# A hybrid decoder layer on one core: odd heads' probability scales and all ALiBi biases moved to the scalar engine

## The chip, the cores and the metric

The kernel runs on one core of a Trainium2 chip. The metric is the device time of one execution in microseconds (us), as the median of several runs. Engines are named as in the profile: PE is TensorE (matmuls; its weight loads are listed as PEld), DVE is VectorE, ACT is ScalarE, POOL is GpSimd, SP is SyncE, which issues the DMAs.

## What is computed

One decoder layer on x of 512 tokens by 1024 features, in float32. Cut to its steps:

```
h = rmsnorm(x, attn_norm)
mq, mk, mv, rq, rk, rv, rg = split(h @ w_in)             # 7 parts of 512 columns
moba = block-sparse causal attention(mq, mk, mv)         # 8 heads of 64, blocks of 256 keys
       softmax(q k^T / 8 - slope_h * distance) @ v       # slope_h = 2^-(h+1), h = 0..7
ret  = chunkwise retention(rq, rk, rv)                   # 4 heads of 128, decay per head
ret  = head_groupnorm(ret) * silu(rg)
x = x + concat(moba, ret) @ w_out
h = rmsnorm(x);  u = causal conv of width 3 (h @ w_up)   # 2816 wide
x = x + (gelu(u) * (h @ w_gate)) @ w_down
x = x + (p @ w_ple) * sigmoid(rmsnorm(x) @ w_ple_gate)
out = rmsnorm(x, final_norm)
```

With 512 tokens there are two blocks of 256 keys, so that every query sees all keys up to its own.

## The kernel before

Activations are kept transposed, features on partitions and the 512 tokens along the free axis. Every float32 product is made of three float32r matmuls: each operand is split into a rounded part `hi` and the remainder `lo`, and `mm3` issues hi·hi (L93), hi·lo of the moving side (L94) and lo·hi (L95). Operand names ending in `h` and `l` are the two parts.

A weight comes by DMA as a raw tile `wr`, ACT rounds it into `wh` (L152), and the remainder `wl = wr - wh` is made on POOL for the keys mv, rq, rk, rg, mq, mk and out, on DVE for the others (L153, L154). The `wh` and `wl` buffers are four each, so a `wh` waits until PE is through with the weight that had its buffer.

`project` (L359) makes one 128-feature tile of a projection: 24 matmuls into a PSUM tile `pj`, a scaling copy `pt` on DVE (L366), then a split, `hi` on ACT (L75) and `lo` on DVE (L82).

Retention goes head by head. `ret_scores` (L408) makes four score tiles; each is multiplied by its decay on DVE (`rt`, L420), rounded on ACT (L422) and the remainder made on DVE (L423). The last tile of a head goes into two fixed tiles called `corner`, the others into `rh` and `rl`. `ret_values` (L426) multiplies them with the values into `ro`.

MoBA goes through g = 0 to 3, two heads each (e = 0 and 1, so that head h is 2g + e), with two blocks b of queries each and two steps in each block: sixteen steps, in which the score rows of both heads have 128, 256, 384 or 512 keys. `softmax` adds the bias and takes the minimum of the negated row in one DVE instruction (`ml`, L458, listed as CUSTOM_DVE_ANT_0), Exp and the row sum on ACT (L461; `me` are the probabilities, `mt` the sum), the reciprocal on DVE (`mi`, L463), and scales the probabilities by it on DVE, in place (L464). `moba_turn` then transposes the probabilities on PE into a PSUM tile `mp` and splits it, `hi` on ACT (L512), `lo` on DVE (L513); the tiles on the diagonal go into other fixed `corner` tiles, the rest into `mph` and `mpl`. `moba_values` multiplies them with the values into `mo`, and adds the two halves through a copy `mr` on ACT (L530) and a sum `mt` on DVE (L531).

The bias of a head is `base`, a tile of distances, times 2^-(h+1): one instruction of 128x512 on POOL (L453). The biases of heads 0 and 1 are issued in the second round of the retention loop, after its three projections (L629 to L631), and those of heads 2g + 2 and 2g + 3 at the end of `moba_scores` for block 0 of g.

Between the steps the schedule puts other work of PE as a fill: projections, and products of the output projection `ou` (L610 to L668). The order of PE's instructions is fixed as written, by a dependency of each on the one before (L843 to L850). The orders on DVE, ACT and POOL are made by the scheduler of the tile framework, which estimates durations and moves an instruction ahead of another that is expected to be ready later. Each engine then works through its list in that order. Eight PSUM tiles and 76 tiles of 128x512 in the on-chip memory are handed out in turn, so an instruction may also wait until a tile's last reader is through.

Of the kernel before, what the change touches and what calls it, by code (L numbers as in the profile page):

```python
# [13 lines left out]
AF = mybir.ActivationFunctionType  # L14
ALU = mybir.AluOpType
# [26 lines left out]
def hybrid_layer_kernel(ctx, tc, x, p, attn_norm, w_in, ret_norm, w_out, ffn_norm, w_up, w_gate,  # L42
                        conv_w, conv_b, w_down, ple_norm, w_ple, w_ple_gate, final_norm, decay, out):
    nc = tc.nc
# [15 lines left out]
    def h2k(s, dt=F32):  # L60

        return heap.tile([P, T], dt, tag="b2k", name=nm(s))
# [4 lines left out]
    def sm(s, n=4, dt=F32):  # L67
        return small.tile([P, n], dt, tag=f"sm{n}", name=nm(s), bufs=12)
# [255 lines left out]
    base = h2k("base")  # L324
# [7 lines left out]
    for kk in range(4):  # L332
# [13 lines left out]
        for h in range(HR):  # L346
            nc.vector.tensor_scalar(c[:, h * DR:(h + 1) * DR], a[:, h * DR:(h + 1) * DR], mean[:, h:h + 1], None,
                                    op0=ALU.subtract)
# [100 lines left out]
    biases, probs, probsT, pair = {}, {}, {}, {}  # L449

    def moba_bias(h):
        biases[h] = h2k("bias")
        nc.gpsimd.tensor_scalar(biases[h], base, 2.0 ** -(h + 1), None, op0=ALU.mult)  # L453

    def softmax(s, h, qt, e):
        keys = P * (qt + 1)
        least = sm("ml", 1)
        nc.vector.tensor_tensor_reduce(e, s[:, :keys], biases[h][:, T - keys:], scale=-1.0,  # L458
                                       scalar=3.4e38, op0=ALU.add, op1=ALU.min, accum_out=least)
        total = sm("mt", 1)  # L460
        nc.scalar.activation(e, e, AF.Exp, bias=least, scale=-1.0, accum_out=total)  # L461
        inv = sm("mi", 1)
        nc.vector.reciprocal(inv, total)  # L463
        nc.vector.tensor_scalar(e, e, inv, None, op0=ALU.mult)  # L464

    def moba_scores(g, b, step):
        q, (kh, kl) = qs["mq", g], qs["mk", g]
        if step == 0:
            probs[g, b] = {}
            if b == 0:  # L470
                pair[g] = [h2k("me") for _ in range(2)]
        pr, both = probs[g, b], pair[g]
        for qt in (2 * b + step,):
            keys = P * (qt + 1)
            wide = max(keys, 256)
            ss = [ps("ms") for _ in range(2)]
            own = slice(qt * P, (qt + 1) * P)
            for e in range(2):
                nc.tensor.matmul(ss[e][:, :wide], q[e][:, own], kh[e][:, :wide], start=True, stop=False)
                nc.tensor.matmul(ss[e][:, :wide], q[e][:, own], kl[e][:, :wide], start=False, stop=True)  # L480
            for e in range(2):
                if b == 0:
                    pr[e, qt] = both[e][:, qt * P:qt * P + keys]
                else:
                    pr[e, qt] = h2k("me")[:, :keys]
                softmax(ss[e], 2 * g + e, qt, pr[e, qt])
        if step == 0:
            return
        if b == 1:
            del qs["mq", g], qs["mk", g], pair[g]  # L490
            for e in range(2):
                del biases[2 * g + e]
        elif g + 1 < HM // 2:
            for e in range(2):
                moba_bias(2 * g + 2 + e)
# [122 lines left out]
    for h in range(HR):  # L618
        ret_scores(h)
        project(*tiles[3 * h])  # L620
        ret_values(h)
        if h == 0:
            moba_v(3)
        if h:
            ret_gate(h - 1)
        project(*tiles[3 * h + 1])
        ret_sums(h)
        project(*tiles[3 * h + 2])
        if h == 1:  # L629
            for e in range(2):  # L630
                moba_bias(e)  # L631
# [172 lines left out]
    for c in range(2):  # L804
        for t in range(NT):
# [24 lines left out]
            else:  # L830
                nc.scalar.activation(o[0], x3[t, 0], AF.Copy, scale=r4)
                for q in range(2):
                    v = slice(q * 256, (q + 1) * 256)
                    nc.vector.scalar_tensor_tensor(o[1][:, v], x3[t, 1][:, v], r4, fn[1][:, v],
                                                   op0=ALU.mult, op1=ALU.mult)
# [49 lines left out]
```

## Time and profile before

| | us |
|---|---|
| median of three runs | 703.02 |
| lowest and highest run | 702.95, 703.88 |
| the profiled execution | 702.89 |
| its span in the trace | 700.9 |
| mean granted PE clock | 0.994 |
| PE busy | 682.1 |
| DVE busy | 435.1 |
| ACT busy | 284.5 |
| POOL busy | 125.0 |

The span goes from the first to the last instruction of the trace; 2.0 us of the execution's time lie around it. A busy time is the sum of an engine's instructions. PE's clock is given as a share of its full speed: 1.00 is the upper of its two levels, 0.50 the lower. Durations of single instructions overlap a little, since the next one starts before the last result of the one before is written.

### The profile page before, as it was taken

The page shows a single profiled execution, that of the slowest core. Times are in us where ns is not written, and L with a number is a line of the kernel's source. Part 1 is how long each engine was busy: PE and PEld are TensorE (multiplying, and loading weights), DVE is VectorE, ACT ScalarE, POOL GpSimd, SP SyncE. Part 2 cuts the span into 40 slices and gives each one's busy share as a digit, 9 for nine tenths or more (in the row PEclk, how much of TensorE's full clock was granted, in tenths as well). Part 3 has the DMA queues.
Part 4 walks back from the last instruction along what each step waited for, and adds up shares of the span by engine and source line. Part 5 has one row for each costly group of instructions (what it writes and reads, how often), then busy time and mean ns, then how long its engine had stood idle before and what let it go on. Part 6 is the DMA issues. An engine that isn't in the chain of part 4 may idle for free.

```text
span 700.9 us, 8468 instructions
## 1 busy us (share of the span) xinstructions
PE 682.1 (97%) x3200; PEld 568.5 (81%) x3200; DVE 435.1 (62%) x785; ACT 284.5 (41%) x460; POOL 125.0 (18%) x99
## 2 busy tenths in 40 slices
PE   8999999999998999999999999999999999999995
PEld 6888888888776888888888888888888888888884
DVE  5776687766768766775656653234565565466496
ACT  5534633335455764453433431222343343344311
POOL 5236244425425210000000000000000000000145
PEclk9999999999999999999999999999999999999998
DMA  8334422245953012232331222233323212344003
GB/s 269 126 93 133 131 80 75 61 124 147 277 142 92 1 62 59 64 118 75 105 121 60 91 90 91 91 120 121 99 82 121 74 62 75 113 146 163 1 1 120
DMA packets 73390, 71.38 MB, mean 102 GB/s; under 512 B 2450, under 2 KB 62726, under 8 KB 73350
## 3 DMA queue, kind: packets, MB, share of 16 engines
q1 hardware_dynamic: 73190, 70.58, 33.3%
q8 instruction: 25, 0.41, 0.3%
q10 hardware_dynamic: 160, 0.27, 0.1%
q14 instruction: 15, 0.12, 0.1%
HBM read 62.97 MB, written 2.10 MB: 93 GB/s over the span
## 4 chain that ended last, share of the span: by engine, by line
PE 87%; DVE 5%; DMA 2%; ACT 2%; issue 2%; POOL 1%; SPq 0%; DVEq 0%; ACTq 0%; POOLq 0%
PE gate L93 6%; PE gate L95 6%; PE up L95 6%; PE dn L94 6%; PE dn L95 6%; PE gate L94 6%; PE up L93 6%; PE up L94 6%; PE dn L93 6%; PE pj L93 4%; PE pj L94 4%; PE pj L95 4%; PE ou L93 2%; PE ou L95 2%; PE ou L94 2%
## 5 line engine op out<-in xcount | busy, mean ns | idle before, releaser
L152 ACT ACTIVATE wh<-wr 128x1024 fp32r<-128x1024 f32 (+2 forms) x108 | 105.3, 979 | 206.6 <-PE dn L94 57.3
L154 DVE TENSOR_TENSOR wl<-wr,wh 128x1024 fp32r<-128x1024 f32 (+2 forms) x78 | 84.6, 1086 | 45.6 <-ACT wh L152 45.5
L154 POOL TENSOR_TENSOR wl<-wr,wh 128x1024 fp32r<-128x1024 f32 x30 | 73.4, 2447 | 130.0 <-ACT wh L152 130.0
L93 PE MATMUL gate<-h2h,wh 128*128 128x512 f32 x176 | 68.7, 390 | 0.0
L95 PE MATMUL gate<-h2h,wl 128*128 128x512 f32 x176 | 68.5, 389 | 0.0
L94 PE MATMUL gate<-h2l,wh 128*128 128x512 f32 x176 | 68.5, 389 | 0.0
L93 PE MATMUL up<-h2h,wh 128*128 128x512 f32 x176 | 68.5, 389 | 0.0
L94 PE MATMUL up<-h2l,wh 128*128 128x512 f32 x176 | 68.5, 389 | 0.0
L95 PE MATMUL up<-h2h,wl 128*128 128x512 f32 x176 | 68.5, 389 | 0.0
L93 PE MATMUL dn<-ach,wh 128*128 128x512 f32 x176 | 68.5, 389 | 0.0
L94 PE MATMUL dn<-acl,wh 128*128 128x512 f32 x176 | 68.5, 389 | 0.0
L95 PE MATMUL dn<-ach,wl 128*128 128x512 f32 x176 | 68.5, 389 | 0.0
L93 PE MATMUL pj<-h1h,wh 128*128 128x512 f32 x160 | 63.3, 395 | 0.3 <-DVE corner L513 0.3
L94 PE MATMUL pj<-h1l,wh 128*128 128x512 f32 x160 | 62.4, 390 | 0.0
L95 PE MATMUL pj<-h1h,wl 128*128 128x512 f32 x160 | 62.4, 390 | 0.0
L711 POOL MEMSET u<- 128x2 f32 x22 | 2.1, 100 | 316.4 <-DVE c L718 316.4
L722 DVE TENSOR_TENSOR ga<-gate,r2b 128x512 f32<-128x512 f32 x22 | 15.2, 691 | 41.3 <-PE gate L95 41.3
L712 DVE TENSOR_TENSOR u<-up,r2b 128x512 f32<-128x512 f32 x22 | 15.1, 692 | 40.1 <-PE up L95 40.1
L94 PEld LDWEIGHTS up<-h2l,wh 128*128 128x128 f32 x176 | 33.0, 188 | 6.9
L93 PEld LDWEIGHTS dn<-ach,wh 128*128 128x128 f32 x176 | 33.0, 188 | 6.9
L94 PEld LDWEIGHTS dn<-acl,wh 128*128 128x128 f32 x176 | 33.0, 188 | 6.9
L95 PEld LDWEIGHTS gate<-h2h,wl 128*128 128x128 f32 x176 | 33.0, 188 | 6.9
(234 smaller groups left out, 1416.0 us busy)
## 6 DMA issues: line engine op xcount, KB each, us to landing
wr<-in_w_up_dram SPq DMA_DIRECT2D x11, 1024.0 KB, 5.4
wr<-in_w_gate_dram SPq DMA_DIRECT2D x11, 1024.0 KB, 5.4
wr<-in_w_in_dram SPq DMA_DIRECT2D x20, 512.0 KB, 4.0
wr<-in_w_down_dram SPq DMA_DIRECT2D x8, 768.0 KB, 4.3
wr<-in_w_down_dram SPq DMA_DIRECT2D x8, 640.0 KB, 4.1
wr<-in_w_ple_gate_dram SPq DMA_DIRECT2D x4, 1024.0 KB, 4.9
wr<-in_w_out_dram SPq DMA_DIRECT2D x3, 1024.0 KB, 6.2
xn<-in_x_dram SPq DMA_DIRECT2D x8, 256.0 KB, 5.8
```

Of the source, the lines that this page charges most:

```text
L93: nc.tensor.matmul(acc, a[0], b[0], start=first, stop=False)
L94: nc.tensor.matmul(acc, a[0], b[1], start=False, stop=False)
L95: nc.tensor.matmul(acc, a[1], b[0], start=False, stop=last)
L152: nc.scalar.activation(hi, part, AF.Copy)
L154: (nc.gpsimd if aside else nc.vector).tensor_tensor(lo, part, f(hi), op=ALU.subtract)
L711: nc.gpsimd.memset(u[:, 0:2], 0.0)
L712: nc.vector.tensor_tensor(u[:, 2:], up, r2b, op=ALU.mult)
L722: nc.vector.tensor_tensor(ga, gate, r2b, op=ALU.mult)
```

## The change

`moba_bias` makes the bias by an ACT copy with a scale in place of a POOL multiplication, for all eight heads. In `softmax` the heads with odd h (e = 1) scale their probabilities by an ACT copy, with the reciprocals as the scale of each row; the even heads keep the DVE multiplication. So one scale of each of the sixteen steps moves from DVE to ACT, four each of 128, 256, 384 and 512 columns. No data, tile or DMA is added. Lines behind L464 stand three lines further down in the changed kernel (the L512 of before is L515).

```diff
     def moba_bias(h):
         biases[h] = h2k("bias")
-        nc.gpsimd.tensor_scalar(biases[h], base, 2.0 ** -(h + 1), None, op0=ALU.mult)
+        nc.scalar.activation(biases[h], base, AF.Copy, scale=2.0 ** -(h + 1))
...
         inv = sm("mi", 1)
         nc.vector.reciprocal(inv, total)
-        nc.vector.tensor_scalar(e, e, inv, None, op0=ALU.mult)
+        if h % 2:
+            nc.scalar.activation(e, e, AF.Copy, scale=inv)
+        else:
+            nc.vector.tensor_scalar(e, e, inv, None, op0=ALU.mult)
```

PE's and SP's lists are the same before and after. ACT's and DVE's lists change in order too. Three places follow, all on ACT; a row with + is of the changed kernel alone, one with - of the kernel before, the others of both.

First, ACT in the third head of the retention (`rh`, and `corner_610` for its last score tile); `wh_1408` is a weight of a later projection:

```order
 L369 ACTIVATE sil_1159<-pt_1157 128x512
+L453 ACTIVATE bias_1161<-base_419 128x512
+L453 ACTIVATE bias_1163<-base_419 128x512
 L422 ACTIVATE rh_1173<-rt_1171 128x512
 L422 ACTIVATE rh_1183<-rt_1181 128x384
 L422 ACTIVATE rh_1193<-rt_1191 128x256
+L152 ACTIVATE wh_1408<-wr_1268 128x1024
 L422 ACTIVATE corner_610<-rt_1201 128x128
-L152 ACTIVATE wh_1408<-wr_1268 128x1024
 L75 ACTIVATE rqh_1236<-pt_1234 128x512
```

The two biases are new ahead of `rh_1173`, and `wh_1408` has moved ahead of `corner_610`. On DVE, at the same place, the copy `pt_1234` of a projection has moved ahead of `corner_611`, the remainder that belongs to `corner_610`.

Second, ACT at the change from g = 0 to g = 1 of MoBA: `me_1781` are probabilities of head 1, `me_1839` and `me_1840` those of heads 2 and 3, `corner_602` a turned tile, `wh_2116` a weight of the output projection:

```order
 L152 ACTIVATE wh_2112<-wr_2008 128x1024
 L461 ACTIVATE me_1781,mt_1784<-me_1781,ml_1782 128x512
-L512 ACTIVATE corner_602<-mp_1941 128x384
+L465 ACTIVATE me_1781<-me_1781,mi_1786 128x512
+L515 ACTIVATE corner_602<-mp_1941 128x384
 L461 ACTIVATE me_1839,mt_1849<-me_1839,ml_1847 128x128
 L461 ACTIVATE me_1840,mt_1856<-me_1840,ml_1854 128x128
 L75 ACTIVATE mqh_1890<-pt_1886 128x512
+L465 ACTIVATE me_1840<-me_1840,mi_1858 128x128
+L152 ACTIVATE wh_2116<-wr_2110 128x1024
 L461 ACTIVATE me_1839,mt_1906<-me_1839,ml_1904 128x256
-L152 ACTIVATE wh_2116<-wr_2110 128x1024
```

Two scales are new, ahead of `corner_602` and behind `mqh_1890`, and `wh_2116` has moved ahead of an Exp of 256 columns. DVE's list has at this place, before and after, the reciprocal that needs this Exp ahead of the minimum of `me_1840`.

Third, ACT in the first two steps of g = 2: `me_2154` and `me_2155` are probabilities of heads 4 and 5, `corner_606` a turned tile, `mr_2248` a copy in `moba_values`:

```order
+L465 ACTIVATE me_2155<-me_2155,mi_2173 128x128
 L461 ACTIVATE me_2154,mt_2221<-me_2154,ml_2219 128x256
-L530 ACTIVATE mr_2248<-mo_2237 64x256
+L453 ACTIVATE bias_2233<-base_419 128x512
+L453 ACTIVATE bias_2235<-base_419 128x512
+L533 ACTIVATE mr_2248<-mo_2237 64x256
 L152 ACTIVATE wh_2768<-wr_2336 128x1024
 L461 ACTIVATE me_2155,mt_2228<-me_2155,ml_2226 128x256
-L512 ACTIVATE corner_606<-mp_2286 128x384
```

The next row of ACT after these is `corner_606` in the changed kernel as well (L515). A scale and two biases are new ahead of it, the biases ahead of `wh_2768` too.

## Rows read from the trace of the kernel before

**Rows 1.** The page, part 1: each engine's busy us, share of the span, instructions

```profile
PE 682.1 (97%) x3200; PEld 568.5 (81%) x3200; DVE 435.1 (62%) x785; ACT 284.5 (41%) x460; POOL 125.0 (18%) x99
```

**Rows 2.** PE's waits: line waited for, us in total, times, longest

```profile
PE ou L93 <- DVE corner L513: 3.1, 1, 3.1
PE ou L93 <- DVE ml L458: 1.7, 1, 1.7
...
PE mo L522 <- DVE mpl L513: 1.2, 1, 1.2
```

**Rows 3.** Groups by line and shape: busy us, mean ns, idle before and its releasers

```profile
L464 DVE TENSOR_SCALAR me<-me,mi 128x384 f32<-128x384 f32 x8 | 3.4, 424 | 0.0
...
L461 ACT ACTIVATE me<-me,ml 128x512 f32<-128x512 f32 x8 | 5.8, 719 | 4.4 <-DVE ml L458 3.5 <-DVE me L464 0.9
L461 ACT ACTIVATE me<-me,ml 128x384 f32<-128x384 f32 x8 | 4.9, 616 | 4.1 <-DVE ml L458 3.8 <-DMA mq<-mqh 0.3
...
L461 ACT ACTIVATE me<-me,ml 128x128 f32<-128x128 f32 x8 | 3.2, 401 | 4.1 <-DVE ml L458 4.1
```

**Rows 4.** Timeline of 115 to 124 us (retention): start, us, instruction, idle before

```profile
115.11 2.40 POOL L154 TENSOR_TENSOR wl<-wr,wh 128x1024 fp32r<-128x1024 f32 x1 [1.06 <-ACT wh L152]
...
116.26 1.80 DVE L423 TENSOR_TENSOR rl<-rt,rh 128x512 fp32r<-128x512 f32 x1 [0.70 <-ACT rh L422]
...
120.89 0.39 PE L94 MATMUL pj<-h1l,wh 128*128 128x512 f32 x1
...
121.28 0.31 ACT L422 ACTIVATE corner<-rt 128x128 fp32r<-128x128 f32 x1 [0.75 <-DVE rt L420]
...
121.49 1.04 ACT L152 ACTIVATE wh<-wr 128x1024 fp32r<-128x1024 f32 x1
...
121.62 0.29 DVE L423 TENSOR_TENSOR corner<-rt,corner 128x128 fp32r<-128x128 f32 x1 [0.44 <-ACT corner L422]
...
122.61 2.40 POOL L154 TENSOR_TENSOR wl<-wr,wh 128x1024 fp32r<-128x1024 f32 x1 [5.11 <-ACT wh L152]
...
123.03 0.28 PE L94 MATMUL ro<-corner,rvh 128*128 128x256 f32 x1
```

**Rows 5.** Timeline of 181 to 192 us (first MoBA steps)

```profile
182.58 2.36 POOL L154 TENSOR_TENSOR wl<-wr,wh 128x1024 fp32r<-128x1024 f32 x1 [7.86 <-ACT wh L152]
...
183.44 1.78 DVE L464 TENSOR_SCALAR me<-me,mi 128x512 f32<-128x512 f32 x1
...
187.83 0.51 ACT L461 ACTIVATE me<-me,ml 128x256 f32<-128x256 f32 x1 [0.22 <-DVE ml L458]
...
188.55 0.40 DVE L458 CUSTOM_DVE_ANT_0 me<-ms,bias 128x256 f32<-128x256 f32 x1
...
189.53 2.41 POOL L154 TENSOR_TENSOR wl<-wr,wh 128x1024 fp32r<-128x1024 f32 x1 [1.40 <-ACT wh L152]
...
189.85 0.40 PE L93 MATMUL pj<-h1h,wh 128*128 128x512 f32 x1
...
190.41 0.56 DVE L513 TENSOR_TENSOR corner<-mp,corner 128x384 fp32r<-128x384 f32 x1
```

**Rows 6.** Timeline of 212 to 222 us (MoBA, g = 2)

```profile
213.51 2.95 POOL L453 TENSOR_SCALAR bias<-base 128x512 f32<-128x512 f32 x2
...
215.58 0.68 DVE L82 TENSOR_TENSOR mql<-pt,mqh 128x512 fp32r<-128x512 f32 x1
...
216.92 2.50 DVE L464 TENSOR_SCALAR me<-me,mi 128x256 f32<-128x256 f32 x1
216.93 2.35 POOL L154 TENSOR_TENSOR wl<-wr,wh 128x1024 fp32r<-128x1024 f32 x1 [0.47 <-ACT wh L152]
...
217.38 0.49 ACT L512 ACTIVATE corner<-mp 128x384 fp32r<-128x384 f32 x1
...
219.80 0.55 DVE L513 TENSOR_TENSOR corner<-mp,corner 128x384 fp32r<-128x384 f32 x1
```

**Rows 7.** A stretch behind the longest wait: us, PE, PEld, DVE, ACT, POOL, clock, DMA, GB/s

```profile
220.80:224.20 3.40, 3.40 (x10) 2.62 (x9) 2.86 (x7) 2.40 (x5) 1.28 (x1) 0.50 0.89 294
```

## The prediction

> **What bounds the kernel now.** I read the page first: PE is busy 682.1 us, 97% of the span, 3200 matmuls [rows 1]. So PE paces, and an edit on ACT, DVE or POOL counts only where PE comes to wait, or stops waiting. The waits of PE, read next, are few, and the largest three lie in MoBA: 3.1 us for a `corner` lo part, 1.7 us for a softmax minimum, 1.2 us for a turned lo part [rows 2]. The change can take away at most these 6.0 us. What they pull after them is read from the table by stretches: behind the 3.1 us wait PE's granted clock stands at half speed for 3.4 us [rows 7]. Behind the 1.7 and 1.2 us waits I found no such stretch. A stretch of 3.4 us at half speed does 1.7 us of work, so the large wait costs 3.1 + 1.7 = 4.8 us. Last come the timelines around each wait and around the places where the order of instructions changes: the reader is to see there which engine releases PE, and what that engine did just before.
>
> The rows show a second thing: while POOL works on a weight's lo part, some DVE instructions stand still. The retention's `rl` (512 columns, both inputs in SBUF) was listed at 116.26 beside POOL's `wl` of 115.11 to 117.51 and took 1.80 us [rows 4]; a DVE subtraction of the same size with both inputs in SBUF took 0.68 [rows 6]. A probability scale of 256 columns took 2.50 us beside a `wl` [rows 6], one of 512 took 1.78 [rows 5]. Each ended within some 0.6 us of POOL's end. A `corner` lo part that subtracts from PSUM was not held: it took 0.56 at 190.41, inside POOL's `wl` of 189.53 to 191.94 [rows 5].
>
> **The change part by part.** A new price first: an ACT scale by a per-row factor. The nearest rows are ACT's own Exp of the same sizes: 0.40 us for 128 columns, 0.62 for 384, 0.72 for 512 [rows 3]; I take these. On DVE 384 columns took 0.42 [rows 3]. A bias of 512 columns on ACT is priced by plain copies: 0.31 us for 128 columns [rows 4], 0.49 for 384 [rows 6], so about 0.58 for 512; I take 1.1 for a pair. In all 16 scales leave DVE, one in each step, four of each size, and 8 biases leave POOL.
>
> That each scale is dearer on ACT costs 0.62 − 0.42 = 0.19 us at 384 columns, 16 × 0.19 = 3.0 us if every one lay on PE's path. ACT was busy 41% of the span [rows 1], so I cost the scales at nothing except at the places below; if that cover were gone, 3.0 us is the price. The Trainium skill, page "ScalarE: Activation LUTs", section "Rules for kernel authors", speaks against the change: a multiplication belongs on VectorE, up to about three times faster per element in bf16. The trace has 1.45 times (0.62 against 0.42, in float32); at three times the estimate for the 16 would be 6.6 us instead of 3.0.
>
> *Retention, 121 to 125 us: +2.1.* The first two biases now stand on ACT ahead of `rh_1173` (first piece of the order, above). They cost nothing: `rl`, which needs `rh`, could start at 116.26 but stood held by POOL until 117.51 [rows 4], which covers 1.25 us, and the pair is 1.1. If that `wl` were not there, the pair would reach DVE in full, 1.1 us. The dear part is the exchange of `wh_1408` and `corner_610`. Before, `corner` hi ran at 121.28, `wh` behind it at 121.49, POOL's `wl` at 122.61, and the lo part at 121.62 on DVE was through before POOL began [rows 4]. Now `wh` comes first. It needs its buffer, free when PE's product of 120.89 ends (121.28), so it runs 121.3 to 122.3; POOL's `wl` starts 0.1 behind it, about 122.4, as 122.61 stands to 121.49 + 1.04 [rows 4]. `corner` hi then runs 0.31 and ends near 122.6, and DVE's lo part, two SBUF inputs, comes about 0.2 us behind POOL's start: held until 122.4 + 2.4 = 124.8, done at about 125.1. PE's product with it was due at 123.03 [rows 4]: 2.1 us late. Ends: 0 (it slips in ahead of POOL) and 2.3 (`wh` starts 0.2 later, at 121.49 as before). I take 2.1, since POOL is ahead by most of the estimates. A wait of 2.1 lies nearer 1.7 (clock kept) than 3.1 (clock lost), so I add nothing for the clock; the other end is +1.7.
>
> *First MoBA steps, 181 to 192: −0.5.* The DVE scale at 183.44, held 1.78, is an odd head's and goes; with it goes the 1.7 us wait [rows 2, 5]. But ACT now holds that scale (0.7) ahead of `corner` hi, another of 128 columns (0.4), and `wh_2116` (1.04) ahead of the Exp of 256 columns (second piece). That Exp ran at 187.83; DVE's next reciprocal waits for it, and behind that on DVE stands the other head's minimum of 188.55, which gives PE a PSUM bank for the projection started at 189.85 [rows 5]. The delays sum to 0.7 + 0.4 + 1.0 = 2.1; the slack is 189.85 − 188.95 = 0.9. So a new wait of 1.2 takes the place of 1.7. Ends: −1.7 (no new wait) and +0.4 (no slack). I take −0.5.
>
> *The turned lo part near 197: +0.2.* Its 1.2 us wait [rows 2] is for a split that ends behind DMAs out of `mq`, and two biases (1.1) now stand on ACT just ahead of that. Ends 0 and +1.1; I take 0.2, nearer nothing, because a DMA ends that wait and not ACT.
>
> *217 to 220: −0.5.* DVE's even-head scale of 216.92 was held by the `wl` of 216.93, and `corner` lo stood behind it until 219.80, though its hi part had begun at 217.38 [rows 6]. Now two biases and a scale stand on ACT ahead of `wh` (third piece), so `wl` starts some 1.1 later and that DVE scale runs before it, unheld. `corner` hi however comes behind the biases, the `wh` and an Exp: 217.38 + 1.1 plus 0.3 to 0.6 for the scale and for gaps begins near 218.9; its lo part, which reads PSUM and so is not held, follows near 219.35 in place of 219.80 [rows 6], some 0.5 earlier. Ends: −3.1 (ACT hides all) and +0.6 (a whole scale more). With the wait still at 2.6, nearer 3.1 than 1.7, I leave the clock's 1.7 us in on both sides.
>
> *The rest: +0.2.* The other twelve or so scales and the other biases meet PE without waits in the rows; one `corner` late in MoBA comes behind an ACT scale. Ends 0 and 1.0.
>
> The sum: +2.1 − 0.5 + 0.2 − 0.5 + 0.2 = +1.5. The profiled execution took 702.89, so 704.4; the median of the runs stands 0.13 above it, so **704.5**. Some 0.2% of the time, 1.4 us, is what a measurement can tell from no change.
>
> **The rivals.**
>
> *A, DVE gets in first at 122.6.* Then POOL is the one that waits, the 2.1 us are gone: 704.5 − 2.1 = 702.4. For it: the margin is 0.2 us. Against it: at 216.92 DVE was listed 0.01 ahead of POOL and was held all the same [rows 6].
>
> *B, the clock stays up at 217* because the idle stretch shrinks from 3.1 to 2.6: 704.5 − 1.7 = 702.8. The rows have a fall behind 3.1 and none behind 1.7; 2.6 lies between.
>
> *C, the clock falls at 123 as well*, behind 2.1 us of idle PE: 704.5 + 1.7 = 706.2. The same rows leave it open.
>
> *D, ACT paces MoBA.* If half of the 16 scales lie on PE's path, 1.5 us more: 706.0. For it: in each step ACT must now do Exp, Exp and scale before the turn. Against it: ACT is busy 41% [rows 1].
>
> *E, faster: the emptied queues clear 217.* If `corner` hi gets ahead of the biases there, it starts at about 217.4, PE waits some 1.5 instead of 3.1 and the clock stays up: −1.6 − 1.7. If the first steps also keep slack, −1.7 in place of −0.5. With the +2.1 of retention and 0.4 of small terms, 703.0 − 1.6 − 1.7 − 1.7 + 2.1 + 0.4 = 700.5. It decides where `corner` hi begins: before 217.6 or not. The order now puts it behind the biases, which speaks against. That freeing POOL of biases frees DVE as well would speak for it, but a subtraction with two SBUF inputs ran in 0.68 at 215.58, inside POOL's biases of 213.51 to 216.46 [rows 6]. The Trainium skill, page "SBUF — State Buffer", section "SBUF: two separate sides", has DVE and GpSimd exclude each other for a whole instruction, for any GpSimd operation that reads SBUF. By it that subtraction would have been held; the trace disagrees for the biases and agrees for `wl`. If it held for the biases too, E would deserve more.
>
> That the change does not do what it says is excluded: the order shows the instructions on ACT, none on the old engines.
>
> **How the numbers follow.** Chances: the forecast 0.40, A 0.15, B 0.13, C 0.12, D 0.10, E 0.10. The forecast's own range is 703.8 to 705.2, so its lower half, 0.18, falls within 1.4 us of the time before, its upper half, 0.22, beyond. Same: 0.18 + A + B = 0.46. Slower: 0.22 + C + D = 0.44. Faster: E, 0.10. The range goes from A to C, 702.4 to 706.3; it leaves out E and the tails of A and D.
>
> **What would show it.** Right: a new wait of about 2 us of PE for the DVE `corner` of the retention near 123, with POOL's `wl` beside that instruction; the 1.7 us wait gone and one of about 1.2 for a minimum in its place near 188; the 3.1 us wait at 2.4 to 2.8, half speed behind it; ACT busy some 14 us more, POOL 12.1 less; ACT scales near 0.4 to 0.7 us. Wrong: no wait at 123; a wait at 217 below 2 us; the clock at half speed elsewhere; or waits of PE for ACT in most steps.

## The result, and the profile after

The change makes the kernel slower: 707.88 us median of six runs (706.15 to 710.79) against 702.99 for the kernel before, a ratio of 1.0070 with a 95% interval of 1.0047 to 1.0093. Measured once more later (e4 below) it took 706.09 us, a ratio of 1.0050 (1.0027 to 1.0074). The forecast was 704.5, with a range up to 706.3: the sign of its sum is right, its size, +1.5, is too small against the +4.9 measured here and the +3.8 of e4. One of the eight runs of e9 (below) took 2385.30 us at a mean granted clock of 0.28 and is left out of e9's median.

The page of the changed kernel, part 1, against [rows 1]: PE has 2.7 us more of busy time, with the same matmuls; DVE and POOL lost 9.5 and 12.3 us, ACT gained 10.6.

```profile
PE 684.8 (97%) x3200; PEld 571.4 (81%) x3200; DVE 425.6 (60%) x769; ACT 295.1 (42%) x484; POOL 112.7 (16%) x91
```

The new instructions' groups, by line and shape. The prices taken from the Exp rows were right: 0.39, 0.61 and 0.72 us for 128, 384 and 512 columns [rows 3].

```profile
L453 ACT ACTIVATE bias<-base 128x512 f32<-128x512 f32 x8 | 4.6, 617 | 0.0
L465 ACT ACTIVATE me<-me,mi 128x512 f32<-128x512 f32 x4 | 2.9, 722 | 0.3 <-DVE mi L463 0.2
L465 ACT ACTIVATE me<-me,mi 128x384 f32<-128x384 f32 x4 | 2.5, 613 | 1.0 <-DVE mi L463 1.0
...
L465 ACT ACTIVATE me<-me,mi 128x128 f32<-128x128 f32 x4 | 1.6, 394 | 1.8 <-DVE mi L463 1.8
```

PE's waits, against [rows 2]:

```profile
PE ou L93 <- DVE corner L516: 2.5, 1, 2.5
PE mo L525 <- DVE mpl L516: 2.3, 1, 2.3
PE ro L94 <- DVE corner L423: 1.9, 1, 1.9
...
PE xt L223 <- DMA xn<-in_x_dram: 0.9, 1, 0.9
...
PE pj L93 <- DVE ml L458: 0.8, 1, 0.8
```

The 1.7 us wait for a minimum is gone, one of 1.9 for the retention's corner tile is new, one of 0.8 for another minimum is new, and the wait for the turned lo part has grown from 1.2 to 2.3.

The retention, in the timeline of the changed kernel (start, us, instruction, idle before), against [rows 4]:

```profile
122.44 1.06 ACT L152 ACTIVATE wh<-wr 128x1024 fp32r<-128x1024 f32 x1 [0.89 <-PE pj L94]
...
123.41 0.29 ACT L422 ACTIVATE corner<-rt 128x128 fp32r<-128x128 f32 x1
...
123.58 2.35 POOL L154 TENSOR_TENSOR wl<-wr,wh 128x1024 fp32r<-128x1024 f32 x1 [4.98 <-ACT wh L152]
...
123.73 2.35 DVE L423 TENSOR_TENSOR corner<-rt,corner 128x128 fp32r<-128x128 f32 x1 [0.42 <-ACT corner L422]
...
126.13 0.39 PE L94 MATMUL ro<-corner,rvh 128*128 128x256 f32 x1 [1.86 <-DVE corner L423]
```

This is the row that the forecast named: DVE's 128 columns, 0.29 us before, take 2.35, because POOL began 0.15 us earlier.

Then 185 to 202 us. PE is released at 192.16 by the minimum that stands behind ACT's `wh`; what decides is lower down, at the copies of `mq`. In the kernel before, ACT had rounded a turned tile (`mph`) at 192.97, and only the lo part waited for the copies, until 196.90:

```profile
181.52 3.19 SPq L573 DMA_DIRECT2D wpr<-in_w_ple_dram  x4
...
187.64 1.41 SPq L380 DMA_DIRECT2D mq<-mqh  x2
...
192.97 0.58 ACT L512 ACTIVATE mph<-mp 128x512 fp32r<-128x512 f32 x1
...
196.90 0.69 DVE L513 TENSOR_TENSOR mpl<-mp,mph 128x512 fp32r<-128x512 f32 x1 [3.37 <-DMA mq<-mqh]
...
197.64 0.38 PE L522 MATMUL mo<-corner,mv 128*128 128x256 f32 x1 [1.24 <-DVE mpl L513]
```

In the changed kernel the rounding waits for the copies as well, until 199.57, and the lo part comes behind it:

```profile
190.12 1.15 SPq L380 DMA_DIRECT2D mq<-mqh  x2
...
192.16 0.50 PE L93 MATMUL pj<-h1h,wh 128*128 128x512 f32 x1 [0.82 <-DVE ml L458]
...
199.57 1.09 ACT L515 ACTIVATE mph<-mp 128x512 fp32r<-128x512 f32 x2 [3.70 <-DMA mq<-mqh]
200.41 0.69 DVE L516 TENSOR_TENSOR mpl<-mp,mph 128x512 fp32r<-128x512 f32 x1 [4.07 <-DMA mq<-mql]
...
201.15 0.58 PE L525 MATMUL mo<-corner,mv 128*128 128x256 f32 x1 [2.33 <-DVE mpl L516]
```

So PE starts 1.58 us after the copies first let an engine go on, where before it was 0.74. The trace shows these waits, not their reason; tiles are handed out in turn, so the split may have been given tiles that the copies still read.

And 220 to 225 us, against [rows 6]: ACT's corner tile comes behind the biases and `wh`, as forecast; its lo part is not held.

```profile
220.25 1.14 ACT L453 ACTIVATE bias<-base 128x512 f32<-128x512 f32 x2
...
221.69 1.04 ACT L152 ACTIVATE wh<-wr 128x1024 fp32r<-128x1024 f32 x1
...
223.25 0.49 ACT L515 ACTIVATE corner<-mp 128x384 fp32r<-128x384 f32 x1
...
223.77 0.56 DVE L516 TENSOR_TENSOR corner<-mp,corner 128x384 fp32r<-128x384 f32 x1 [0.35 <-ACT corner L515]
```

The table by stretches of the changed kernel (columns as in [rows 7]) shows half clock at two places, the first one new:

```profile
202.00:204.00 2.00, 2.00 (x11) 2.00 (x11) 1.22 (x5) 0.71 (x2) 2.00 (x1) 0.50 0.00 0
...
224.40:228.00 3.60, 3.60 (x9) 2.88 (x10) 3.06 (x6) 2.67 (x6) 1.96 (x2) 0.55 0.40 108
```

Set side by side matmul by matmul, the two profiled executions (spans 700.9 and 705.3) part like this: +0.9 us in the first 10 us, +2.2 at 123, −1.75 at 185, +0.95 at 189, +1.2 at 197, +1.1 in the half clock behind it, −0.65 at 217, +0.4 at 255; in all +4.4.

### The profile page after: what moved, and what is told of

It reads as the page before. It is cut to its first block, busy times and chain, and to the rows that moved or that the text cites. A ratio compares the mean times of both kernels' runs of the same rounds, so it can differ in the third digit from the quotient of the medians.

```text
span 705.3 us, 8430 instructions
## 1 busy us (share of the span) xinstructions
PE 684.8 (97%) x3200; PEld 571.4 (81%) x3200; DVE 425.6 (60%) x769; ACT 295.1 (42%) x484; POOL 112.7 (16%) x91
## 4 chain that ended last, share of the span: by engine, by line
PE 89%; DVE 5%; ACT 2%; DMA 2%; issue 1%; POOL 1%; SPq 0%; DVEq 0%; ACTq 0%; POOLq 0%
PE gate L93 6%; PE gate L94 6%; PE dn L94 6%; PE up L94 6%; PE gate L95 6%; PE up L95 6%; PE dn L95 6%; PE dn L93 6%; PE up L93 6%; PE pj L93 5%; PE pj L94 4%; PE pj L95 4%; PE ou L93 2%; PE ou L95 2%; PE ou L94 2%
## 5 line engine op out<-in xcount | busy, mean ns | idle before, releaser
L93 PEld LDWEIGHTS up<-h2h,wh 128*128 128x128 f32 x176 | 33.0, 188 | 6.9
L93 PEld LDWEIGHTS gate<-h2h,wh 128*128 128x128 f32 x176 | 33.1, 188 | 6.8
```

The lines of the kernel that those rows point to most:

```text
L93: nc.tensor.matmul(acc, a[0], b[0], start=first, stop=False)
```

## The experiments

Two theories stood. *Places*: the change costs where PE waits, by an order on ACT that lets POOL hold DVE at 123, and by transfers that land late at 197, with the clock behind. *ACT's price*: each scale on ACT lengthens its step. The kernel before ran beside each group of runs.

| run | median us | before beside it | ratio (95%) |
|---|---|---|---|
| e1 scales alone | 701.51 | 702.32 | 0.9983 (0.9959 to 1.0006) |
| e2 biases alone | 705.39 | 702.32 | 1.0035 (1.0013 to 1.0057) |
| e3 change, first pair on POOL | 703.47 | 702.32 | 1.0020 (0.9995 to 1.0045) |
| e4 change again | 706.09 | 702.32 | 1.0050 (1.0027 to 1.0074) |
| e5 change, order back | 703.65 | 702.54 | 1.0017 (0.9998 to 1.0035) |
| e6 change, late loads | 703.52 | 702.54 | 1.0008 (0.9990 to 1.0026) |
| e7 scales alone, late loads | 698.55 | 702.54 | 0.9940 (0.9924 to 0.9956) |
| e8 before, late loads | 700.90 | 702.54 | 0.9971 (0.9954 to 0.9988) |
| e9 change, both repairs | 701.25 | 702.41 | 0.9966 (0.9942 to 0.9989) |
| e10 as e7 | 698.01 | 702.41 | 0.9937 (0.9920 to 0.9954) |

**The two halves of the change (e1, e2).** From the changed kernel, e1 puts the biases back:

```diff
-        nc.scalar.activation(biases[h], base, AF.Copy, scale=2.0 ** -(h + 1))
+        nc.gpsimd.tensor_scalar(biases[h], base, 2.0 ** -(h + 1), None, op0=ALU.mult)
```

> The odd heads' scales on ACT as in the change, all biases back on POOL. Theory of places (the change costs where PE comes to wait: 2.2 us at 123 from the first pair of biases, which turns the order of the weight's rounding and the corner tile; at 185 to 201 what PE gains is taken back by a transfer that lands late): no wait of PE for the corner tile at 123, the wait of 1.7 us at 185 gone, the wait near 197 for the turned lo part longer than 1.2 us (about 2), in all between -0.6 and +1.5 us against the kernel before. Rival (each scale on ACT lengthens the chain of its step, since ACT is the dearer place): most of the change's loss, +2.5 us or more.

e2 puts the scales back:

```diff
-        if h % 2:
-            nc.scalar.activation(e, e, AF.Copy, scale=inv)
-        else:
-            nc.vector.tensor_scalar(e, e, inv, None, op0=ALU.mult)
+        nc.vector.tensor_scalar(e, e, inv, None, op0=ALU.mult)
```

> All biases on ACT as in the change, all scales on DVE. Theory of places: the wait of about 2 us at 123 with DVE's corner instruction at about 2.4 us, the 1.7 us wait at 185 still there, no change of more than 0.6 us at 217; +1.5 to +2.7 us. Rival (the scales cost): within 0.6 us of the kernel before.

The scales alone are 0.8 us below the kernel before by the medians, 0.2 below the range that was expected and not separable from no change; the biases alone carry 3.1 us. So it is not the price of scales on ACT. PE's waits in e1:

```profile
PE mo L525 <- DVE mpl L516: 1.9, 1, 1.9
PE ou L93 <- DVE corner L516: 1.7, 1, 1.7
```

No wait at 123, 1.7 us gained at 185, and 1.9 us lost at 197 in place of 1.2; at 217 PE waits 1.7 us in place of 3.1, with no half clock behind it (none between 20 and 670 us). PE's waits in e2:

```profile
PE ou L93 <- DVE corner L513: 3.5, 1, 3.5
PE ro L94 <- DVE corner L423: 1.9, 1, 1.9
PE ou L93 <- DVE ml L458: 1.7, 1, 1.7
```

Here the wait at 197 has vanished: PE came 2 us late from 123, and the transfers had time. The 3.1 us lie above the 2.7 that was the high end expected. In the profile the wait at 217 grew by 0.4 only, but the half clock behind it lasted from 219.5 to 226.4, twice as long as before.

**Which biases (e3), and the chance in a single run (e4).**

```diff
-        nc.scalar.activation(biases[h], base, AF.Copy, scale=2.0 ** -(h + 1))
+        if h < 2:
+            nc.gpsimd.tensor_scalar(biases[h], base, 2.0 ** -(h + 1), None, op0=ALU.mult)
+        else:
+            nc.scalar.activation(biases[h], base, AF.Copy, scale=2.0 ** -(h + 1))
```

> The change, with only the biases of heads 0 and 1 back on POOL. Theory of places: no wait at 123, the rest as in the change, so 2.2 us less than the change: +1.3 to +2.7 against the kernel before. Rival (the scales cost): as the change, +3.5 to +5.

> The change itself on this chip. +3.5 to +5.5 us against the kernel before. In the first profile its first 10 us were 0.9 us longer with the same instructions; if that is chance of the transfers at the start, it isn't so in each of these four profiles; if it belongs to the change, it is here again and not in the run with the scales alone.

With the first pair back on POOL the corner tile stands ahead of `wh` again, the wait at 123 is gone, and 2.6 us with it (706.09 to 703.47), so that e3 is +1.2, just below the low end of what was expected. In the trace of e3, though, the wait at 197 has grown: PE, no longer late, stands 2.8 us there.

```profile
PE mo L528 <- DVE mpl L519: 2.8, 1, 2.8
PE ou L93 <- DVE corner L519: 2.5, 1, 2.5
```

The execution of e4 that was profiled took 702.50, at the bottom of its range: the same three waits as in the first profile, 2.5, 1.9 and 1.7 us, and no half clock behind any of them. Over the ten runs of e4 the time goes with the clock: 702.50 us at a mean granted clock of 0.996, 708.41 at 0.989. Their clocks have a mean of 0.9918, those of the 31 runs of the kernel before beside them 0.9935; by that, as an estimate, 0.0017 of 703 us, 1.2 of the 3.8 us, lie in the clock.

The start was 0.2 us longer than in the profile before, against 0.9 in the first one; over all profiles here, whose first 10 us hold the same instructions, it is between −0.4 and +1.6. So that 0.9 does not belong to the change. Nor is it the wait for `xn` in the list of waits above: e10 waits 1.5 us there and is only 0.2 late behind it. In the first profile of the change PE's matmuls of 128x512 take some 0.63 us until 9.4 us and 0.40 from 9.8, in the kernel before 0.40 from 6.8.

**The order alone (e5).** Biases and scales stay on ACT; one order is forced back:

```diff
-    issued, halved = [0], [0]
+    issued, halved, marks = [0], [0], {}
...
                 nc.scalar.activation(hi, part, AF.Copy)
+                if n_of["wh"] == 18:
+                    marks["wh"] = last_of(mybir.EngineType.Activation)
...
             nc.scalar.activation(hi[:, own:], t[:, own:], AF.Copy)
+            if h == 2 and kt == NT - 1:
+                marks["corner"] = last_of(mybir.EngineType.Activation)
...
+    tc.add_manual_dep(marks["wh"], marks["corner"].name, mybir.DependencyInfo(
+        mybir.DependencyClass.NoSync, mybir.DependencyReason.DATA), reason="program order")
```

> The change, with one order on ACT forced back: the corner tile's rounding ahead of the weight's rounding in the third retention head. All biases and scales stay on ACT. If the order of these two is what costs (POOL's remainder then holds DVE's corner instruction): no wait of PE at 123, DVE's corner instruction back to about 0.3 us, and 1 to 2 us less than the change in all, +1.5 to +2.8 against the kernel before, since part of the 2 us returns as a longer wait near 197. If the time of the two biases on ACT costs: a wait of 1 us or more stays at 123.

The timeline of e5 at that place:

```profile
122.84 0.31 ACT L424 ACTIVATE corner<-rt 128x128 fp32r<-128x128 f32 x1 [0.75 <-DVE rt L422]
123.06 1.04 ACT L152 ACTIVATE wh<-wr 128x1024 fp32r<-128x1024 f32 x1
...
123.77 0.28 DVE L427 TENSOR_TENSOR corner<-rt,corner 128x128 fp32r<-128x128 f32 x1
124.18 2.39 POOL L156 TENSOR_TENSOR wl<-wr,wh 128x1024 fp32r<-128x1024 f32 x1 [5.04 <-ACT wh L152]
```

DVE is through before POOL begins, and PE doesn't wait, with both biases still on ACT. So it is the order, not the biases' time. Measured: +1.1 us against the kernel before, just below the +1.5 that was the low end expected, where e4 stood at +3.8. As expected, part of the gain returns at 197; the profile, which is of e5's longest run (706.02 us), has the clock at half behind this wait, from 199.3 to 206.1:

```profile
PE mo L529 <- DVE mpl L520: 3.0, 1, 3.0
```

**The transfers (e6, e7, e8).** The loads of w_ple and p, 1.5 MB, stood in SP's queue ahead of the `mq` copies. One line asks for them a round later:

```diff
-        if i == 1:
+        if i == 2:
             ple_load()
```

e6 is the change with that, e7 the scales alone with that, e8 the kernel before with that.

> The change, with the 1.5 MB of loads for the last stage (w_ple and p) asked for one round of the MoBA loop later, so that the copies of mq stand ahead of them in the DMA queue. If the queue of transfers from 175 to 197 us sets when PE goes on at 197: the wait near 197 gone, and 1.7 to 3 us less than the change, about +0.5 to +2 against the kernel before. If ACT or DVE is what is late there: the wait stays at about 2 us.

> The scales alone on ACT, biases on POOL, with the same loads later. If the queue sets the time at 197: the wait of 1.9 us there gone and the gain of 1.75 us at 185 kept, -2 to -3.5 us against the kernel before. If not: as with the scales alone, -0.8.

> The kernel before with the same loads later, nothing else. If the queue sets the time at 197: its wait of 1.2 us there gone, -0.8 to -1.5 us; the waits of 1.7 at 185 and 3.1 at 217 stay. If not: no difference.

In e8 the copies are through 5 us after their issue at 188.97, where in the kernel before ACT and DVE waited for them until 196.90, 9 us after an issue at 187.64. At 197 PE goes on without a wait:

```profile
188.97 1.11 SPq L380 DMA_DIRECT2D mq<-mqh  x2
190.18 1.19 SPq L380 DMA_DIRECT2D mq<-mql  x2
191.46 3.28 SPq L573 DMA_DIRECT2D wpr<-in_w_ple_dram  x4
...
193.99 1.07 ACT L512 ACTIVATE mph<-mp 128x512 fp32r<-128x512 f32 x2
```

The same stretch by the table, for the kernel before and then for e8 (the last columns are the clock, the DMA engines' busy share and GB/s):

```profile
176.00:196.00 20.00, 18.30 (x94) 15.44 (x94) 12.01 (x35) 9.12 (x22) 7.81 (x4) 1.00 0.90 260
```

```profile
176.00:196.00 20.00, 19.76 (x104) 16.53 (x103) 14.80 (x42) 10.87 (x27) 8.27 (x5) 1.00 0.77 223
```

With the DMA engines at 0.90 in those 20 us the copies wait behind loads that nobody needs yet. The line is worth 1.6 us to the kernel before, 3.2 to the scales alone (from e1's −0.8 to e7's −4.0 against the kernel before) and 2.8 to the change (from e4's +3.8 to e6's +1.0). e6 came out as expected, e7 and e8 gained 0.5 and 0.1 us more.

Not all of that is the queue. With the line moved, the scheduler also made other orders on DVE and ACT, so e8 changed more than the loads. At 197 itself the profiles gain 1.3 us (e8 against the kernel before), 2.1 (e7 against e1), and 2.4 and the half clock behind it (e6 against the change). In e8 the 1.7 us wait at 185, which was expected to stay, is gone without a moved scale: DVE now has the minimum ahead of the held scale and not behind it. The wait of 3.1 at 217, expected to stay as well, is 2.3 with one of 0.4 just ahead.

```profile
185.06 0.29 DVE L458 CUSTOM_DVE_ANT_0 me<-ms,bias 128x128 f32<-128x128 f32 x1
...
185.28 1.67 DVE L464 TENSOR_SCALAR me<-me,mi 128x512 f32<-128x512 f32 x1
```

The scales' gain, hidden in e1, shows itself: e7 is 4.0 us below the kernel before, and 2.4 below e8. Against e8 it cannot lie at 185, where e8 has no wait either. It lies at 217, where DVE's scale for the even head stood beside POOL's `wl` in e8:

```profile
215.91 2.52 DVE L464 TENSOR_SCALAR me<-me,mi 128x256 f32<-128x256 f32 x1
215.93 2.36 POOL L154 TENSOR_TENSOR wl<-wr,wh 128x1024 fp32r<-128x1024 f32 x1 [0.53 <-ACT wh L152]
```

and was through before it in e7:

```profile
216.27 0.34 DVE L467 TENSOR_SCALAR me<-me,mi 128x256 f32<-128x256 f32 x1
...
216.78 2.38 POOL L154 TENSOR_TENSOR wl<-wr,wh 128x1024 fp32r<-128x1024 f32 x1 [0.83 <-ACT wh L152]
```

PE waits 0.8 and 0.3 us there in e7, and the half clock that e8 has from 219.7 to 223.1 is absent.

**Both repairs (e9), and the best kernel again (e10).** e9 is the change with the edits of e5 and e6, e10 is the kernel of e7.

> The change with both repairs: the corner tile's rounding ahead of the weight's on ACT in the third retention head, and the loads of w_ple and p one round later. If the two places and the clock behind them are what the change costs: no wait at 123 and none near 197, about 2 us less than with the late loads alone, -0.5 to -2 us against the kernel before, and still 2 to 3 us above the scales alone with the late loads, for what the biases on ACT cost at 217. If the scales on ACT cost by themselves: not below the kernel before.

> The scales alone on ACT, with the late loads, once more beside the kernel with both repairs: -3 to -4.5 us against the kernel before; PE's wait at 217 below 1 us and no stretch of half clock behind it.

e9 is 1.2 us below the kernel before by the medians, where e6 was 1.0 above it, and has no wait at 123 or 197, as expected. e10 repeats e7: 4.4 us below the kernel before, faster than both kernels of this document. What still lies between e9 and e10, 3.2 us, are the biases on ACT and one more order edit. PE's waits near 217 in e9:

```profile
PE ms L486 <- DVE ml L462: 1.5, 1, 1.5
...
PE ou L93 <- DVE corner L520: 0.7, 1, 0.7
```

and in e10:

```profile
PE ou L93 <- DVE corner L516: 0.8, 1, 0.8
...
PE ms L482 <- DVE ml L458: 0.2, 1, 0.2
```

With the biases on ACT it is 2.2 us and the clock is at half from 219.3 to 222.8; without them 1.0 us, and no half clock up to 670 us.

## Why the prediction was wrong, step by step

- **What bounds the kernel.** Right: PE paces, and, the start apart, nearly all of the time came and went at the waits that were named and in the clock behind them.
- **The price of a scale and a bias on ACT.** Right to 0.04 us. The new groups sum to 13.6 us, as forecast, while ACT's busy time rose by 10.6: it counts a stretch where one instruction overlaps the next only once, and all durations of ACT added up rose by 13.4. That the scales lie beside other work is right too: e1 is no slower than the kernel before. Rival D falls. The rule that a multiplication belongs on VectorE, from the Trainium skill, page "ScalarE: Activation LUTs", section "Rules for kernel authors", agrees with the single instruction (0.61 against 0.42 us) and not with the kernel: e7 with its sixteen dearer scales is 2.4 us below e8, with DVE's scale at 217 no longer beside POOL (0.34 us in place of 2.52).
- **Retention, +2.1.** Right: 2.2 in the profile, with the instruction, its holder and the duration as worked out, and e5 shows the cause. Rival A falls: DVE was held in every profile with this order (the change twice, e2, e6), though POOL was ahead by 0.15 us only. Rival C didn't come at 123: in none of these four did the clock fall there.
- **First MoBA steps, −0.5.** Right in both parts: −1.75 for the scale that is gone, +0.95 for the minimum behind `wh_2116`, −0.8 in all.
- **The turned lo part, +0.2.** This step failed. It read "I take 0.2, nearer nothing, because a DMA ends that wait and not ACT". The first half is what the trace says; the conclusion does not follow from it. In the profile the wait grew by 1.1 us. Counted from its stand ahead of 185, PE came here 0.7 us earlier, by what the step before had gained, and the copies let the first engine go on only 0.4 earlier. The larger part, 0.8, is ACT's: its rounding, which before had run ahead of the copies' end, now stood behind them. So the step named the wrong work of ACT. It is not the two biases, since e1, which has none on ACT, shows the same: in the change, e1, e3, e4 and e5 it is 1.4 to 1.6 us from the copies to PE's start, against 0.74 before. The step's upper end, 1.1, was about the size of the growth, but it hung on the biases and left out the clock. What else the wait hangs on, the runs showed: where PE comes late, it's gone (e2), and 1.5 MB of loads further back in the queue remove it from every kernel (e6 to e8). No run moves the rounding alone, so its share is read from the profiles and not shown by an experiment.
- **The clock, nothing added.** The second failure. I allowed for a fall at 123, rival C, and gave it no place at 197. In the profile it fell there, behind 2.3 us of idle PE, and cost 1.1 us; over the runs of e4 the estimate from the granted clock is 1.2. Rival B was open as well, and stayed open: at 217 the clock stayed up in e3, e4 and e5 and fell in the profile of the change, each behind 2.5 us.
- **217 to 220, −0.5.** Right: −0.65, with the wait at 2.5. Rival E falls: ACT's corner tile began behind the biases.
- **The rest, +0.2.** +0.4, at 255.

Without the start, the profile moved by +3.5; the forecast of +1.5 lacks 1.0 at 197, 1.1 of clock, and is off by 0.1 to 0.3 in four terms that nearly cancel out. The other 0.9 of the profile is the start, which varies by itself. The range was too narrow at its top because the 197 term's ends left out the clock behind it, and because each rival was priced alone.

## What to carry to other kernels

What is gained ahead of a wait that a transfer ends is kept only as far as the transfer, and all that stands behind it, comes earlier too. Here 0.6 to 0.9 us were gained between 185 and 190 in the change, e1, e3, e4 and e5, and 0.5 to 1.8 lost again at 197. So look, behind every place where a change gains, for the next wait that a DMA ends, for what stands ahead of that DMA in its queue, and for which engines stand behind it. And where a scheduler makes the order, compare the order before pricing the instructions, for an edit that moves only a load too: a pair of copies of 1.1 us cost nothing by itself here, and 2 us by the exchange of two others.

## What the runs showed of the hardware beyond what was expected

PE's clock fell behind some idle stretches and not behind others of nearly the same length. In the profiles above, from 120 to 260 us, it never fell behind a wait of 1.9 us or less standing alone (1.9 at 123 in the change, twice, and in e2 and e6; 1.7 at 185 before and in e2; 1.9 at 197 and 1.7 at 217 in e1; 1.7 at 197 in e4), and it fell behind each of 2.8 or more (e3 and e5 at 197, the kernel before and e2 at 217). Of six waits of 2.3 to 2.5 us three were followed by a fall (the change at 197 and 217 in the first profile, e8 at 217) and three were not (e3, e4 and e5 at 217), so that two profiles of the same kernel, the change, differ at 217. In e6 and e9 the clock fell there behind waits of 1.5 and 0.7 us close together. It also fell near the start in e5, e8 and e9, from about 8 to 11 us, where PE had waited 1.7, 0.8 and 0.9 us for `xn`. Each fall lasted some 3.4 us or twice that; the one at 197 in the change cost 1.1 us. The runs of e4 lie between 702.50 and 708.41, those of e7, whose profile has no fall between 11 and 670 us, between 697.41 and 699.59. What decides stays open.
